# Two-layer hybrid trunk in split fp32: more block products by the seven-product scheme, their block sums by DMA, output projections by pairs of column blocks

## The chip, the cores and the metric

The kernel runs on one core of one Trainium2 chip. The metric is the device time of one execution in microseconds (us). Lower is better.

## The reference

What is computed, for 256 tokens (two tiles of 128, here called t = 0 and 1), a model width of 2048 and a hidden width of 5632, all in float32:

```
for layer in range(2):
    h = rmsnorm(x, g_mix[layer])
    if layer == 0:
        p = h @ w_in_ab                      # 2048 -> 3072
        a = gmlp_mixer(p[..., :2048])        # gelu, norm, 128-token spatial gating
        b = multi_scale_pool(p[..., 2048:])  # trailing means over 2, 4, 8, 16 tokens
        mix = concatenate([a, b]) @ w_out_ab # 2048 -> 2048
    else:
        mix = mla(h, ...)                    # attention over low-rank q and kv, ending in o @ w_out_c
    x = x + mix
    h = rmsnorm(x, g_ffn[layer])
    x = x + (silu(h @ w_gate) * (h @ w_up)) @ w_down   # 2048 -> 5632 -> 2048
out = rmsnorm(x, g_final)
```

## The kernel before

**Split products.** TensorE multiplies in a rounded 32-bit format, so every weight tile is split in two: ACT copies it to its rounded part `wh` (L105) and DVE subtracts to get the rest `wl` (L106). Activations are split in the same way. One product of a 128x128 activation block with a 128x512 weight block is three matmuls (L211, L212, L213 in `token_product`): hi by wh, hi by wl, lo by wh.

**Quads.** In the feed-forward network (FFN) the weights come as quads of 2048 columns (1 MiB): two blocks of 128 rows of the product by two blocks of 512 columns, b11, b12, b22, b21. With the two token tiles of the left side, a quad is a product of 2x2 blocks by 2x2 blocks. Done plainly ("eight") it is 8 block products, 24 matmuls. Done by the scheme of Strassen and Winograd ("seven") it is 7 block products, 21 matmuls, which go to eight PSUM banks: c11, c12, c21, c22 (pool "mm") and p1, p6, p5, p7 (pool "sm"), joined by DVE adds when the column pair ends. A seven needs sums of blocks: on the left s1, s2, s4 (made once, in `split_pair`), on the right t13 = (b11+b12, b12+b22), 1024 columns wide, and t2, t4 (512 each, L253). `SEVEN` names the quads (3, 5, 6 and 7 of the eight of a column pair of gate and up) that go by seven products, `SEVEN_DOWN` those of down: 3 and 5 of eight, in the last part 3 of six.

**Where t13 comes from.** For quads in `SUMMED` (3, 6, 7 of gate/up) `sums_of` makes it with two DMAs on GpSimd's queue into one of two `t13` buffers: L573 writes src[:, :1024], L574 adds src[:, 512:1536] (512 KB each). The second waits for the first to land, and a first waits until its buffer has been read for the last time, by the split of the t13 two sums before (L106, wl<-t). The other sevens get t13 from one DVE add over 1024 columns (L253, sums<-raw).

**The order.** `chunks_of` is a generator over all quads of a layer's FFN. It starts sums up to three quads, and loads and splits up to two quads (`AHEAD`), before they are used. SP issues one 1 MiB load per quad (L579) into one of three `raw` buffers. An FFN is three parts of (4, 4, 3) chunks. A chunk is one column pair of gate and up (8 quads), its eviction, SiLU, product `hd`, and transposes (L262), which TensorE does after quads 1 and 2 of the next chunk. After a part's chunks comes down: two column pairs of 8 quads (parts 0 and 1), or one pair of 6 quads and two plain column blocks (part 2). `pair_into` evicts a down pair: the p banks after the last seven quad, c11 to c22 at its end (`evict`).

**The output projections** (`w_o0`, `w_o1`, after the mixer and the attention) go through `token_major`: four plain blocks of 512 columns, each 96 matmuls into two banks. After block 2 `trunk_rstd` (L370 and L371 on DVE, L373 and L377 on GpSimd) makes a normalizing factor from the squares (L321) of 1536 columns; ACT scales the trunk by it (L307) and TensorE transposes it (L262) into the FFN's left side during block 3 and at the start of the FFN.

**The start.** The first mixer needs a per-token factor along the free dimension: L191 sums squares by matmul, GpSimd takes the power (L195, `rtok`) and `spread` (L201) turns it on TensorE.

Of the kernel before, what the change touches and what calls it, by code (L numbers as in the profile page):

```python
# [8 lines left out]
F32 = mybir.dt.float32  # L9
# [5 lines left out]
P = 128  # L15
# [8 lines left out]
SUMMED = (3, 6, 7)  # L24

SEVEN_DOWN = {4: (3, 5), 3: (3,)}
# [9 lines left out]
def trunk(ctx: ExitStack, tc: tile.TileContext, a: dict, out: bass.AP):  # L36
# [86 lines left out]

    def next_pending(n=1):
# [159 lines left out]
    def into_trunk(w, k0, nk, moving, g, sums, chunks=None, scaled=None, pairs=None, pair_into=None):  # L284
# [28 lines left out]
        def evict(c, pss):  # L313
            s = slice(c * 512, (c + 1) * 512)
            for t in range(2):
                add(x[:, t, s], pss[t], x[:, t, s])
            if g is None:
                return
            for t in range(2):
                sq = ev([512])  # L320
                nc.scalar.activation(out=sq, in_=x[:, t, s], func=AF.Square, accum_out=sums[:, t, c:c + 1])  # L321
            if g == "final":
                for t in range(2):
                    nc.vector.tensor_tensor(out=x[:, t, s], in0=x[:, t, s], in1=gfin[:, s], op=ALU.mult)
            elif scaled is None:
                for m in (4 * c, 4 * c + 2):
                    pending.append(lambda m=m: turn(m, lambda t, j: x[:, t, (m + j) * P:(m + j + 1) * P]))
            elif c == 2:
                scaled["by"], scaled["back"] = trunk_rstd(sums[:, :, :3], 1536, back=True)
                for b in range(3):  # L330
                    turn_scaled(b)
            elif c == 3:
                turn_scaled(3)

        if pairs is not None:
            for b in pairs:
                pair_into(2 * b, evict)
        blocks = range(4) if pairs is None else range(2 * len(pairs), 4)
# [117 lines left out]
    PAD = 16  # L456
    st, att, qpool = stage(att=1, qpool=2)
# [22 lines left out]
    def pool_product(g):  # L480
        parts = split_weights(a["w_pool"][:, g * 512:(g + 1) * 512], 512)
        wh, wl, _ = parts[0]
        for i in range(2):
            ps = ps_mm.tile([P, 2 * T], F32, name="mm")
            for k in range(2):
                s = slice((i * 2 + k) * P, (i * 2 + k + 1) * P)
                short_product(ps, wh[:, s], wl[:, s], diff[:, 2 * (g % 2) + k, :], k == 0, k == 1)
            m = 2 * g + i
            split_into(ab[:, 8 + m, :], ps[:, :T], gain("pool", m))

    for g in range(4):
        z = qpool.tile([P, 2, PAD + T], F32, name="qn")
        nc.vector.memset(z[:, :, :PAD], 0.0)
        for i in range(2):
            ps = column(a["w_z0"][2 * g + i], KD, xs)
            if rx is None:
                rx = kept(spread(rtok))
            s = gather_halves(ps)
            nc.vector.tensor_tensor(out=z[:, i, PAD:], in0=s, in1=rx, op=ALU.mult)
        pool_group(g, z)  # L500
        if g:
            pool_product(g - 1)

    for m in range(8):

        wb = ev([2, P])
        nc.scalar.dma_start(out=wb, in_=a["w_s"][m])
# [21 lines left out]
    into_trunk(a["w_o0"], 0, KD, ab, "ffn0", sums, scaled=scaled)  # L529


    def quad_seven(raw, t13=None):

        sums = big.tile([P, 2048], F32, name="sums")
        if t13 is None:
            t13 = sums[:, :1024]
            add(t13, raw[:, 512:1536], raw[:, :1024])
        t2, t4 = sums[:, 1024:1536], sums[:, 1536:]  # L540
# [6 lines left out]
        parts += split_raw(sums[:, 1024:], 1024)  # L547
        return dict(zip(("b22", "b21", "b11", "", "t1", "t3", "t2", "t4"), (block(parts, i) for i in range(8))))
# [5 lines left out]
    def chunks_of(layer, early):  # L554

        wgu, wd, we = (a[f"{n}{layer}"] for n in ("w_gu", "w_d", "w_e"))
        quad = lambda j, seven: "seven" if j in seven else "eight"
        todo = []
        at = 0
        for n in PARTS:  # L560
            for c in range(at, at + n):
                todo += [(wgu[c, j], "summed" if j in SUMMED else quad(j, SEVEN)) for j in range(KD // 2)]
            last = at + n == sum(PARTS)
            for b in range(1 if last else 2):
                todo += [(wd[b, 2 * at + j], quad(j, SEVEN_DOWN[n])) for j in range(2 * n)]
            if last:
                todo += [(we[c, :, i * 512:(i + 4) * 512], "whole") for c in range(2) for i in range(0, 4 * n, 4)]
            at += n

        def sums_of(src):  # L570

            t13 = early.tile([P, 1024], F32, name="t13")
            nc.gpsimd.dma_start(out=t13, in_=src[:, :1024])  # L573
            nc.gpsimd.dma_start(out=t13, in_=src[:, 512:1536], accum_op=ALU.add)  # L574
            return t13

        def load(src, kind, t13):
            raw = raws.tile([P, 2 * SPLIT], F32, name="raw")
            nc.sync.dma_start(out=raw, in_=src)  # L579
            if kind == "whole":  # L580
                return split_raw(raw, 2 * SPLIT)
            return quad_eight(raw) if kind == "eight" else quad_seven(raw, t13)
# [54 lines left out]
    def feed_forward(layer, sums, scaled, g_next):  # L637
# [3 lines left out]
        st, hds, early = stage(hds=2, early=2)  # L641
        chunks = chunks_of(layer, early)
        for part, n in enumerate(PARTS):
# [4 lines left out]
            hforms = hds.tile([P, 2, 2, 3, P] if not final else [P, 1, 2, 4, P], F32R, name="hforms", bufs=1)  # L648
            for c in range(n):
# [17 lines left out]
                for t, (g, u) in enumerate(((e11, e12), (e21, e22))):  # L667
                    nc.scalar.activation(out=g, in_=g, func=AF.Silu, scale=f[:, t:t + 1])
                    h = hds.tile([P, 512], F32, name="hd")
                    nc.vector.scalar_tensor_tensor(out=h, in0=u, scalar=f[:, t:t + 1], in1=g, op0=ALU.mult, op1=ALU.mult)  # L670
                    hd.append(h)
# [12 lines left out]
            def pair_into(c, evict, hid=hid, hforms=hforms, seven_d=seven_d):  # L684
                s0, s1 = slice(c * 512, (c + 1) * 512), slice((c + 1) * 512, (c + 2) * 512)
# [23 lines left out]
            into_trunk(None, 0, 4 * n, hid, g_next if final else None, after, chunks, pairs=range(1 if final else 2), pair_into=pair_into)  # L709
# [3 lines left out]

    sums = feed_forward(0, sums, scaled, "mix1")
# [13 lines left out]
    ckv = big.tile([P, 4, 2 * T], F32R, name="ckv")  # L728
    st, att, qpool = stage(att=1, qpool=2)
# [86 lines left out]
    def values(h, prt):  # L816
# [3 lines left out]
        split_into(os_[:, h, :], o[:, :T])  # L820
# [4 lines left out]
    queries, probs = {}, {}  # L825
# [26 lines left out]
    into_trunk(a["w_o1"], 0, KD, os_, "ffn1", sums, scaled=scaled)  # L852
# [8 lines left out]
def _laid_out(i):  # L861
# [15 lines left out]

    def flat(t):
# [17 lines left out]
    o["w_o0"] = wide(i["w_out_ab"][0])  # L896
# [14 lines left out]
    o["w_o1"] = wide(i["w_out_c"][0])  # L911
    for l in range(2):
# [3 lines left out]

        w = i["w_down"][l].reshape(NF // 2, 2, P, 2, 2, 512)
        o[f"w_d{l}"] = np.ascontiguousarray(np.stack([w[:, 0, :, :, 0], w[:, 0, :, :, 1], w[:, 1, :, :, 1], w[:, 1, :, :, 0]]
                                                     ).transpose(3, 1, 2, 0, 4)).reshape(2, NF // 2, P, -1)
# [28 lines left out]
```

## Time and profile before

| | us |
|---|---|
| time, median of 3 runs (lowest to highest) | 1906.62 (1906.11 to 1909.29) |
| the profiled execution's own time | 1904.91 |
| its span in the trace | 1903.1 |
| busy in the span: TensorE (PE) | 1890.4 (99%) |
| VectorE (DVE) | 1584.0 (83%) |
| ScalarE (ACT) | 1149.7 (60%) |
| GpSimd (POOL) | 103.9 (5%) |

A row of the timeline is: start in us, length in us, engine, source line, operation, output and input by the program's names, shapes, number joined in the row, and in brackets the idle time of the engine before it and what ended it. PEld is TensorE's weight load, which runs beside the matmuls. A matmul row's length (0.39) is longer than its step to the next one, since matmuls are pipelined. For POOL's DMA rows the start is the moment of issue.

### The profile page before, as it was taken

What the parts mean: (1) busy time and instruction counts of PE and PEld (TensorE: products, weight loads), DVE (VectorE), ACT (ScalarE), POOL (GpSimd) and SP (SyncE); (2) the same over time, 40 slices, a digit from 0 to 9 for tenths busy, and PEclk for the clock granted to TensorE, in tenths of its full rate; (3) what the DMA queues carried; (4) which work ended last, traced back from release to release, by engine and by line L of the source; (5) the groups of instructions that cost most, each with busy time, mean ns of one, the idle gap of its engine ahead of it and who ended that gap; (6) DMA issues with size and microseconds to landing.
All of it is one profiled execution on the core that took longest, in us unless ns stands there. A gap on an engine that the chain in (4) does not pass through costs nothing. (4 is left out here: it accounts for less than half of the span.)

```text
span 1903.1 us, 24047 instructions
## 1 busy us (share of the span) xinstructions
PE 1890.4 (99%) x8994; PEld 1586.9 (83%) x8994; DVE 1584.0 (83%) x2067; ACT 1149.7 (60%) x1538; POOL 103.9 (5%) x159
## 2 busy tenths in 40 slices
PE   9999999999999999999999999999999999999998
PEld 8888888888888888888889988888888888888886
DVE  7785589998799987999675755899987999978995
ACT  6554676664567654666555755776655667546663
POOL 0000001000011100000000000000100011001000
PEclk9999999999999999999999999999999999999999
DMA  8567568885688865786455255588866888757863
GB/s 310 200 219 240 183 209 291 274 266 208 215 275 274 293 235 192 251 277 237 177 180 182 93 173 194 191 278 285 262 223 208 261 289 269 255 201 254 264 238 127
DMA packets 74277, 440.19 MB, mean 231 GB/s; under 512 B 8496, under 2 KB 10288, under 8 KB 30256
## 3 DMA queue, kind: packets, MB, share of 16 engines
q1 hardware_dynamic: 53136, 364.93, 52.8%
q0 software_dynamic: 19008, 69.21, 15.4%
q10 hardware_dynamic: 2016, 4.51, 0.7%
q8 instruction: 70, 1.15, 0.2%
q14 instruction: 47, 0.39, 0.1%
HBM read 436.52 MB, written 2.10 MB: 230 GB/s over the span
## 5 line engine op out<-in xcount | busy, mean ns | idle before, releaser
L105 ACT ACTIVATE wh<-raw 128x1024 fp32r<-128x1024 f32 (+1 forms) x692 | 669.6, 986 | 470.2 <-PE mm L213 312.3
L106 DVE TENSOR_TENSOR wl<-raw,wh 128x1024 fp32r<-128x1024 f32 (+1 forms) x692 | 772.4, 1133 | 165.8 <-ACT wh L105 163.6
L211 PE MATMUL mm<-wh,xs 128*128 128x512 f32 x880 | 344.0, 391 | 0.7 <-ACT ev L252 0.7
L212 PE MATMUL mm<-wl,xs 128*128 128x512 f32 x880 | 342.5, 389 | 0.0
L213 PE MATMUL mm<-wh,xs 128*128 128x512 f32 x880 | 342.2, 389 | 0.0
L211 PE MATMUL mm<-wh,hid 128*128 128x512 f32 x852 | 333.3, 391 | 0.4 <-ACT ev L252 0.3
L213 PE MATMUL mm<-wh,hid 128*128 128x512 f32 x852 | 332.0, 390 | 0.0
L212 PE MATMUL mm<-wl,hid 128*128 128x512 f32 x852 | 331.7, 389 | 0.0
L105 ACT ACTIVATE wh<-sums 128x1024 fp32r<-128x1024 f32 x146 | 154.8, 1060 | 102.1 <-DVE sums L253 58.4
L106 DVE TENSOR_TENSOR wl<-sums,wh 128x1024 fp32r<-128x1024 f32 x146 | 177.8, 1221 | 28.6 <-ACT wh L105 24.8
L211 PEld LDWEIGHTS mm<-wh,xs 128*128 128x128 f32 x880 | 165.2, 188 | 35.0 <-ACT ev L252 1.2
L213 PEld LDWEIGHTS mm<-wh,xs 128*128 128x128 f32 x880 | 165.2, 188 | 34.3
L212 PEld LDWEIGHTS mm<-wl,xs 128*128 128x128 f32 x880 | 165.3, 188 | 33.6
L211 PEld LDWEIGHTS mm<-wh,hid 128*128 128x128 f32 x852 | 160.0, 188 | 33.7 <-ACT ev L252 0.8
L213 PEld LDWEIGHTS mm<-wh,hid 128*128 128x128 f32 x852 | 160.0, 188 | 33.2
L212 PEld LDWEIGHTS mm<-wl,hid 128*128 128x128 f32 x852 | 160.1, 188 | 32.5
L135 PE MATMUL mm<-xs,wh 128*128 128x512 f32 x375 | 133.8, 399 | 0.0
L106 DVE TENSOR_TENSOR wl<-t,wh 128x1024 fp32r<-128x1024 f32 x66 | 80.6, 1222 | 36.2 <-ACT wh L105 36.2
L136 PE MATMUL mm<-xs,wl 128*128 128x256 f32 x375 | 104.8, 280 | 0.0
L105 ACT ACTIVATE wh<-t 128x1024 fp32r<-128x1024 f32 x66 | 70.0, 1060 | 35.6 <-PE mm L213 29.8
L253 DVE TENSOR_TENSOR ev<-sm,ev 128x512 f32<-128x512 f32 x130 | 83.4, 682 | 2.4 <-ACT ev L252 2.4
L573 POOL DMA_DIRECT2D t<-in_w_gu x66 | 38.9, 590 | 835.2 <-DVE wl L106 718.0
(237 smaller groups left out, 2649.4 us busy)
## 6 DMA issues: line engine op xcount, KB each, us to landing
raw<-in_w_gu SPq DMA_DIRECT2D x176, 1024.0 KB, 5.9
raw<-in_w_d SPq DMA_DIRECT2D x76, 1024.0 KB, 4.9
t<-in_w_gu POOLq DMA_DIRECT2D x132, 512.0 KB, 6.8
raw<-in_w_o SPq DMA_DIRECT2D x32, 1024.0 KB, 4.9
raw<-in_w_e SPq DMA_DIRECT2D x12, 1024.0 KB, 4.9
raw<-in_w_v SPq DMA_DIRECT2D x10, 1024.0 KB, 6.6
raw<-in_w_z SPq DMA_DIRECT2D x8, 1024.0 KB, 4.9
raw<-in_w_u SPq DMA_DIRECT2D x8, 1024.0 KB, 4.9
```

The lines of the kernel that those rows point to most:

```text
L105: nc.scalar.activation(out=wh[:, :m], in_=raw[:, o:o + m], func=AF.Copy)
L106: nc.vector.tensor_tensor(out=wl[:, :m], in0=raw[:, o:o + m], in1=wh[:, :m].bitcast(F32), op=ALU.subtract)
L135: nc.tensor.matmul(ps, lhsT=wh, rhs=mv, start=first, stop=False)
L136: nc.tensor.matmul(ps[:, :T], lhsT=wl, rhs=mv[:, :T], start=False, stop=last)
L211: nc.tensor.matmul(ps, lhsT=hi, rhs=wh, start=first, stop=False)
L212: nc.tensor.matmul(ps, lhsT=hi, rhs=wl, start=False, stop=False)
L213: nc.tensor.matmul(ps, lhsT=lo, rhs=wh, start=False, stop=last)
L253: add = lambda out, p, q: nc.vector.tensor_tensor(out=out, in0=p, in1=q, op=ALU.add)
L573: nc.gpsimd.dma_start(out=t13, in_=src[:, :1024])
```

## The change

- `SEVEN_DOWN` gets one more quad per column pair: 3, 5 and 6 of eight, and 3 and 4 of six.
- Both output projections go by pairs of column blocks, as down does, with quads 4 and 6 (layer 0) or 6 (layer 1) of eight as sevens (`SEVEN_OUT`). Their weights are laid out in quads, and their t13 comes from a DVE add.
- Every seven quad of the FFN, in gate/up and in down, gets its t13 by the two DMAs. A third t13 buffer is the first half of the tile `sums`, which used to be taken anew for each seven; t2 and t4 always use its second half. Of a summed quad SP loads only three quarters, with two DMAs (512 KB and 256 KB), since b12 is not used alone.
- A pair is evicted at its end: first the four adds of c11 to c22, then the p banks.
- `trunk_rstd` of the output projections runs after the first pair, over 1024 columns instead of 1536.
- `hd` is written in place. The loads of `w_s` move from ACT's queue to GpSimd's. The first `spread` comes after the second column of `w_z0` instead of during the first.

```diff
-SUMMED = (3, 6, 7)
-
-SEVEN_DOWN = {4: (3, 5), 3: (3,)}
+
+
+SEVEN_OUT = ((4, 6), (6,))
+SEVEN_DOWN = {4: (3, 5, 6), 3: (3, 4)}
...
-            nc.tensor.matmul(ps, lhsT=wh, rhs=mv, start=False, stop=True)
+            done.append(nc.tensor.matmul(ps, lhsT=wh, rhs=mv, start=False, stop=True))
...
+            complete(c)
+
+        def complete(c):
+            s = slice(c * 512, (c + 1) * 512)
...
-            elif c == 2:
-                scaled["by"], scaled["back"] = trunk_rstd(sums[:, :, :3], 1536, back=True)
-                for b in range(3):
+            elif c == 1:
+                scaled["by"], scaled["back"] = trunk_rstd(sums[:, :, :2], 1024, back=True)
+                for b in range(2):
                     turn_scaled(b)
-            elif c == 3:
-                turn_scaled(3)
-
-        if pairs is not None:
-            for b in pairs:
-                pair_into(2 * b, evict)
-        blocks = range(4) if pairs is None else range(2 * len(pairs), 4)
+            elif c > 1:
+                turn_scaled(c)
 
+        def pair_into(c):
+
+            s0, s1 = slice(c * 512, (c + 1) * 512), slice((c + 1) * 512, (c + 2) * 512)
+
+            def between(j, cs, ps):
+                if begin is not None:
+                    begin(j)
+
+            cs, (p1, p6, p5, p7) = quads(nk // 2, seven, moving, forms, chunks, between)
+
+            for i, ps in enumerate(cs):
+                y = x[:, i // 2, (s0, s1)[i % 2]]
+                add(y, ps, y)
+            u2 = copy(p6)
+            add(x[:, 0, s0], p1, x[:, 0, s0])
+            add(u2, p1, u2)
+            add(x[:, 0, s1], p5, x[:, 0, s1])
+            sub(x[:, 0, s1], x[:, 0, s1], u2)
+            add(u2, p7, u2)
+            add(x[:, 1, s0], x[:, 1, s0], u2)
+            add(x[:, 1, s1], p5, x[:, 1, s1])
+            sub(x[:, 1, s1], x[:, 1, s1], u2)
+            complete(c)
+            complete(c + 1)
...
+            if i == 1:
+                split_pair(ab[:, 7 + m:9 + m, :], both, oforms[:, SEVEN_OUT[0].index((8 + m) // 2)])
...
-            ps = column(a["w_z0"][2 * g + i], KD, xs)
+            waiting.append((i, column(a["w_z0"][2 * g + i], KD, xs)))
             if rx is None:
-                rx = kept(spread(rtok))
-            s = gather_halves(ps)
-            nc.vector.tensor_tensor(out=z[:, i, PAD:], in0=s, in1=rx, op=ALU.mult)
+                if i == 0:
+                    continue
+                with tc.issue_after(done[-1].ins):
+                    rx = kept(spread(rtok))
...
-        nc.scalar.dma_start(out=wb, in_=a["w_s"][m])
+        nc.gpsimd.dma_start(out=wb, in_=a["w_s"][m])
...
+    def quad_seven(raw, t13=None, t24=None):
+
+
+
         if t13 is None:
-            t13 = sums[:, :1024]
+            sums = big.tile([P, 2048], F32, name="sums")
+            t13, t24 = sums[:, :1024], sums[:, 1024:]
             add(t13, raw[:, 512:1536], raw[:, :1024])
...
-                todo += [(wgu[c, j], "summed" if j in SUMMED else quad(j, SEVEN)) for j in range(KD // 2)]
+                todo += [(wgu[c, j], "summed" if j in SEVEN else "eight") for j in range(KD // 2)]
-                todo += [(wd[b, 2 * at + j], quad(j, SEVEN_DOWN[n])) for j in range(2 * n)]
+                todo += [(wd[b, 2 * at + j], "summed" if j in SEVEN_DOWN[n] else "eight") for j in range(2 * n)]
...
+    def out_weights(w, seven):
+        return [(w[b, j], "seven" if j in seven else "eight") for b in range(2) for j in range(KD // 2)]
...
+            both = big.tile([P, 2048], F32, name="sums")
+            begun_sums = []
 
-            t13 = early.tile([P, 1024], F32, name="t13")
+            begun_sums.append(0)
+            t13 = early.tile([P, 1024], F32, name="t13") if len(begun_sums) % 3 else both[:, :1024]
             nc.gpsimd.dma_start(out=t13, in_=src[:, :1024])
             nc.gpsimd.dma_start(out=t13, in_=src[:, 512:1536], accum_op=ALU.add)
             return t13
 
         def load(src, kind, t13):
             raw = raws.tile([P, 2 * SPLIT], F32, name="raw")
-            nc.sync.dma_start(out=raw, in_=src)
+            if kind == "summed":
+
+                nc.sync.dma_start(out=raw[:, 1024:], in_=src[:, 1024:])
+                nc.sync.dma_start(out=raw[:, :512], in_=src[:, :512])
+            else:
+                nc.sync.dma_start(out=raw, in_=src)
...
-                def between(j, cs, ps):
-                    if j != seven_d[-1]:
-                        return
-                    if final and g_next == "final":
-                        nonlocal gfin
-                        gfin = big.tile([P, D], F32, name="sums")
-                        nc.scalar.dma_start(out=gfin, in_=a["g_final"].broadcast_to([P, D]))
-                    p1, p6, p5, p7 = ps
-                    u2 = copy(p6)
-                    add(x[:, 0, s0], p1, x[:, 0, s0])
-                    add(u2, p1, u2)
-                    add(x[:, 0, s1], p5, x[:, 0, s1])
-                    sub(x[:, 0, s1], x[:, 0, s1], u2)
-                    add(u2, p7, u2)
-                    add(x[:, 1, s0], x[:, 1, s0], u2)
-                    add(x[:, 1, s1], p5, x[:, 1, s1])
-                    sub(x[:, 1, s1], x[:, 1, s1], u2)
-
-                (c11, c12, c21, c22), _ = quads(2 * n, seven_d, hid, hforms, chunks, between)
-                evict(c, (c11, c21))
-                evict(c + 1, (c12, c22))
...
-    into_trunk(a["w_o1"], 0, KD, os_, "ffn1", sums, scaled=scaled)
+    into_trunk(None, 0, KD, os_, "ffn1", sums, chunks_of(out_weights(a["w_o1"], SEVEN_OUT[1])), scaled, 2,
+               SEVEN_OUT[1], oforms)
```

In all, TensorE has 48 matmuls fewer, DVE has 104 instructions more although 34 of its 40 adds over 1024 columns are gone, and GpSimd issues 232 DMAs for sums instead of 132.

GpSimd's row of instructions for one chunk of gate and up, the second of layer 0 (t_... is a t13 buffer, in_w_gu the weights of gate and up). Before:

```order
L573 DMA t_2569<-in_w_gu 128x1024
L574 DMA t_2569<-in_w_gu 128x1024
L573 DMA t_2729<-in_w_gu 128x1024
L574 DMA t_2729<-in_w_gu 128x1024
L573 DMA t_2766<-in_w_gu 128x1024
L574 DMA t_2766<-in_w_gu 128x1024
```

And in the changed kernel:

```order
L630 DMA t_2656<-in_w_gu 128x1024
L631 DMA t_2656<-in_w_gu 128x1024
L630 DMA sums<-in_w_gu 128x1024
L631 DMA sums<-in_w_gu 128x1024
L630 DMA t_2816<-in_w_gu 128x1024
L631 DMA t_2816<-in_w_gu 128x1024
L630 DMA t_2853<-in_w_gu 128x1024
L631 DMA t_2853<-in_w_gu 128x1024
```

A chunk has four sums on the queue instead of three, one after the other as before, and the second of them goes to the tile `sums`.

DVE at the place where the trunk's factor is made in the output projection of layer 0 (x is the trunk, mm and sm the PSUM banks, L106 and L107 the weight split, L370 or L403 the reduction for the factor). Before:

```order
L106 TENSOR_TENSOR wl<-raw,wh 128x1024 x8
L253 TENSOR_TENSOR x<-mm,x 128x512 x2
L106 TENSOR_TENSOR wl<-raw,wh 128x1024
L370 TENSOR_REDUCE rstd_s<-tsum 128x2
L371 TENSOR_SCALAR rstd_s<-rstd_s 128x2
L106 TENSOR_TENSOR wl<-raw,wh 128x1024 x2
L279 TENSOR_TENSOR xs<-ev,xs 128x2x256 x2
```

And in the changed kernel, from the add of the last of the four banks on:

```order
L257 TENSOR_TENSOR x<-mm,x 128x512
L257 TENSOR_TENSOR x<-sm,x 128x512 x2
L258 TENSOR_TENSOR x<-x,ev 128x512
L107 TENSOR_TENSOR wl<-raw,wh 128x1024
L257 TENSOR_TENSOR ev<-sm,ev 128x512
L107 TENSOR_TENSOR wl<-raw,wh 128x1024
L257 TENSOR_TENSOR x<-x,ev 128x512
L258 TENSOR_TENSOR x<-x,ev 128x512
L107 TENSOR_TENSOR wl<-raw,wh 128x1024 x2
L403 TENSOR_REDUCE rstd_s<-tsum 128x2
L257 TENSOR_TENSOR sums<-raw 128x1024
L404 TENSOR_SCALAR rstd_s<-rstd_s 128x2
```

Where two adds stood ahead of the reduction, all adds of a pair stand now, with weight splits among them, and a block sum stands between the reduction and the scalar step behind it.

TensorE at the first `spread` (L201, now L205; L191 sums the squares, L135 and L136, now L139 and L140, are a column's products). Before:

```order
L423 MATMUL mm<-wl,xs 128x512
L424 MATMUL mm<-wh,xs 128x512
L191 MATMUL sm<-ones,hid 128x1 x2
L201 MATMUL sm<-ident,rtok 128x128 x2
L135 MATMUL mm<-xs,wh 128x512
L136 MATMUL mm<-xs,wl 128x256
L135 MATMUL mm<-xs,wh 128x512
```

And in the changed kernel:

```order
L139 MATMUL mm<-xs,wh 128x512
L140 MATMUL mm<-xs,wl 128x256
L136 MATMUL mm<-xs,wl 128x256
L137 MATMUL mm<-xs,wh 128x512
L205 MATMUL sm<-ident,rtok 128x128 x2
L139 MATMUL mm<-xs,wh 128x512
L140 MATMUL mm<-xs,wl 128x256
L139 MATMUL mm<-xs,wh 128x512
L140 MATMUL mm<-xs,wl 128x256
```

The turn of rtok has left its place right behind the sums of squares, and stands at the end of the second column.

## Rows read from the trace of the kernel before

**Rows 1.** The page: busy time of the engines, and DMA queues.

```profile
PE 1890.4 (99%) x8994; PEld 1586.9 (83%) x8994; DVE 1584.0 (83%) x2067; ACT 1149.7 (60%) x1538; POOL 103.9 (5%) x159
...
q1 hardware_dynamic: 53136, 364.93, 52.8%
q0 software_dynamic: 19008, 69.21, 15.4%
```

**Rows 2.** Windows: length, busy PE, PEld, DVE, ACT, POOL, clock, DMA share, GB/s.

```profile
295.20:336.90 41.70, 41.70 (x190) 34.62 (x189) 39.17 (x46) 27.38 (x35) 4.21 (x6) 1.00 0.88 278
420.30:462.60 42.30, 42.30 (x188) 35.02 (x187) 37.40 (x43) 21.25 (x24) 0.00 (x0) 1.00 0.65 235
```

**Rows 3.** Timeline of PE: matmuls of a plain block, transposes in a chunk.

```profile
215.63 0.39 PE L211 MATMUL mm<-wh,hid 128*128 128x512 f32 x1
...
217.67 0.39 PE L211 MATMUL mm<-wh,hid 128*128 128x512 f32 x1
...
294.04 1.03 PE L262 MATMUL sm<-ident,hd 128*128 128x128 f32 x8
```

**Rows 4.** Timeline of PE: the first spread.

```profile
51.91 0.71 PE L201 MATMUL sm<-ident,rtok 128*128 128x128 f32 x4 [1.05 <-POOL rtok L195]
```

**Rows 5.** Groups by form: a weight split and a block sum on DVE.

```profile
L106 DVE TENSOR_TENSOR wl<-raw,wh 128x1024 fp32r<-128x1024 f32 x578 | 695.2, 1221 | 149.1 <-ACT wh L105 147.1
...
L253 DVE TENSOR_TENSOR sums<-raw 128x1024 f32<-128x1024 f32 x40 | 48.9, 1222 | 3.9 <-DMA raw<-in_w_gu 3.6
```

**Rows 6.** Timeline of POOL: issues of the sums' DMAs.

```profile
277.38 0.84 POOL L574 DMA_DIRECT2D t<-in_w_gu  x1 [3.72 <-DMA t<-in_w_gu]
278.31 0.56 POOL L573 DMA_DIRECT2D t<-in_w_gu  x1
288.62 0.86 POOL L574 DMA_DIRECT2D t<-in_w_gu  x1 [9.75 <-DMA t<-in_w_gu]
296.62 0.56 POOL L573 DMA_DIRECT2D t<-in_w_gu  x1 [7.14 <-DVE wl L106]
304.00 0.85 POOL L574 DMA_DIRECT2D t<-in_w_gu  x1 [6.83 <-DMA t<-in_w_gu]
...
1235.68 0.85 POOL L574 DMA_DIRECT2D t<-in_w_gu  x1 [3.76 <-DMA t<-in_w_gu]
...
1248.51 0.86 POOL L574 DMA_DIRECT2D t<-in_w_gu  x1 [11.38 <-DMA t<-in_w_gu]
...
1278.92 0.86 POOL L574 DMA_DIRECT2D t<-in_w_gu  x1 [5.36 <-issue]
...
1287.34 0.84 POOL L574 DMA_DIRECT2D t<-in_w_gu  x1 [7.00 <-DMA t<-in_w_gu]
...
1781.28 0.85 POOL L574 DMA_DIRECT2D t<-in_w_gu  x1 [3.85 <-DMA t<-in_w_gu]
...
1793.33 0.84 POOL L574 DMA_DIRECT2D t<-in_w_gu  x1 [10.64 <-DMA t<-in_w_gu]
```

**Rows 7.** The tile t: landing times of its 132 DMAs.

```profile
DMA to landing us min/median/max: 3.9/6.8/13.1
```

**Rows 8.** Timeline of DVE in one chunk: t13 of quad 3, of quad 7.

```profile
295.10 1.22 DVE L106 TENSOR_TENSOR wl<-t,wh 128x1024 fp32r<-128x1024 f32 x1
...
316.63 0.68 DVE L253 TENSOR_TENSOR sums<-t,raw 128x512 f32<-128x512 f32 x1
```

**Rows 9.** Timeline of all engines: end of block 2, first output projection.

```profile
216.71 1.28 DVE L253 TENSOR_TENSOR x<-mm,x 128x512 f32<-128x512 f32 x2
...
219.51 0.16 DVE L370 TENSOR_REDUCE rstd_s<-tsum 128x2 f32<-128x6 f32 x1
...
220.02 0.71 POOL L373 TENSOR_TENSOR rtok<-rstd_s,mhalf 128x2 f32<-128x2 f32 x1 [59.77 <-DVE rstd_s L371]
...
220.92 1.32 ACT L307 ACTIVATE ev<-x,rtok 128x512 f32<-128x512 f32 x2
...
222.44 0.81 PE L262 MATMUL sm<-ident,ev 128*128 128x128 f32 x6
```

More of the change, by code (lines that the diff above doesn't have):

```diff
@@ L282, in split_pair, with into_trunk @@
             nc.vector.tensor_tensor(out=q[:, 1], in0=f, in1=q[:, 0].bitcast(F32), op=ALU.subtract)
-    def into_trunk(w, k0, nk, moving, g, sums, chunks=None, scaled=None, pairs=None, pair_into=None):
+    def into_trunk(w, k0, nk, moving, g, sums, chunks=None, scaled=None, pairs=0, seven=(), forms=None,
+                   begin=None):
         def turn(m, src):
@@ L488, in pool_product @@
             m = 2 * g + i
-            split_into(ab[:, 8 + m, :], ps[:, :T], gain("pool", m))
+            if (8 + m) // 2 not in SEVEN_OUT[0]:
+                split_into(ab[:, 8 + m, :], ps[:, :T], gain("pool", m))
+                continue
+            if i == 0:
+                both = ev([2, T])
+            nc.scalar.activation(out=both[:, i, :], in_=ps[:, :T], func=AF.Copy, scale=gain("pool", m))
+            if i == 1:
+                split_pair(ab[:, 7 + m:9 + m, :], both, oforms[:, SEVEN_OUT[0].index((8 + m) // 2)])
     for g in range(4):
@@ L493, in trunk @@
         nc.vector.memset(z[:, :, :PAD], 0.0)
+        waiting = []
         for i in range(2):
-            ps = column(a["w_z0"][2 * g + i], KD, xs)
+            waiting.append((i, column(a["w_z0"][2 * g + i], KD, xs)))
             if rx is None:
-                rx = kept(spread(rtok))
-            s = gather_halves(ps)
-            nc.vector.tensor_tensor(out=z[:, i, PAD:], in0=s, in1=rx, op=ALU.mult)
+                if i == 0:
+                    continue
+                with tc.issue_after(done[-1].ins):
+                    rx = kept(spread(rtok))
+            for j, ps in waiting:
+                s = gather_halves(ps)
+                nc.vector.tensor_tensor(out=z[:, j, PAD:], in0=s, in1=rx, op=ALU.mult)
+            waiting = []
         pool_group(g, z)
@@ L546, in quad_seven @@
         parts += split_raw(t13, 1024)
-        parts += split_raw(sums[:, 1024:], 1024)
+        parts += split_raw(t24, 1024)
         return dict(zip(("b22", "b21", "b11", "", "t1", "t3", "t2", "t4"), (block(parts, i) for i in range(8))))
@@ L552, in quad_eight, with feed_forward_weights @@
         return dict(zip(("b11", "b12", "b22", "b21"), (block(parts, i) for i in range(4))))
-    def chunks_of(layer, early):
+    def feed_forward_weights(layer):
         wgu, wd, we = (a[f"{n}{layer}"] for n in ("w_gu", "w_d", "w_e"))
-        quad = lambda j, seven: "seven" if j in seven else "eight"
         todo = []
@@ L578, in load @@
             raw = raws.tile([P, 2 * SPLIT], F32, name="raw")
-            nc.sync.dma_start(out=raw, in_=src)
+            if kind == "summed":
[3 more added lines that the diff above has]
+                nc.sync.dma_start(out=raw, in_=src)
             if kind == "whole":
                 return split_raw(raw, 2 * SPLIT)
-            return quad_eight(raw) if kind == "eight" else quad_seven(raw, t13)
+            return quad_eight(raw) if kind == "eight" else quad_seven(raw, t13, both[:, 1024:] if t13 is not None else None)
         count, begun, ready = len(todo), [], []
@@ L640, in feed_forward @@
         at = 0
-        st, hds, early = stage(hds=2, early=2)
-        chunks = chunks_of(layer, early)
+        st, hds, early = stage(hds=1, early=2)
+        chunks = chunks_of(feed_forward_weights(layer), early)
         for part, n in enumerate(PARTS):
@@ L712, in feed_forward @@
         return after
+    into_trunk(None, 0, KD, ab, "ffn0", sums, chunks_of(out_weights(a["w_o0"], SEVEN_OUT[0])), scaled, 2,
+               SEVEN_OUT[0], oforms)
+    outs.close()
     sums = feed_forward(0, sums, scaled, "mix1")
@@ L819, in values @@
         nc.tensor.matmul(o[:, P:T], lhsT=vt[:, 1, h * P:(h + 1) * P], rhs=prt[:, T:384], start=False, stop=True)
-        split_into(os_[:, h, :], o[:, :T])
+        if h // 2 not in SEVEN_OUT[1]:
+            split_into(os_[:, h, :], o[:, :T])
+            return
+        if h % 2 == 0:
+            both.append(ev([2, T]))
+        nc.scalar.activation(out=both[-1][:, h % 2, :], in_=o[:, :T], func=AF.Copy)
+        if h % 2:
+            split_pair(os_[:, h - 1:h + 1, :], both.pop(), oforms[:, SEVEN_OUT[1].index(h // 2)])
     q_tiles = columns(a["w_q"], 4, 24, cq)
-    queries, probs = {}, {}
+    queries, probs, both = {}, {}, []
     for p in range(10):
```

46 lines of the change are left out of this document (30 added, 16 removed).

## The prediction

> **What bounds the kernel now.** The page comes first: TensorE is busy for 1890.4 of 1903.1 us, 99%, and DVE for 83% [rows 1]. So time can be won only by fewer matmuls or by closing the 13 us of gaps; a faster DVE, ACT or DMA gives nothing by itself. The windows then show where a new wait could arise. In a stretch as long as one chunk of gate and up, 41.70 us, TensorE never rests, but DVE is busy for 39.17 and the DMA engines for 0.88 of the time. In a stretch of down they have more room: 37.40 of 42.30, and 0.65 [rows 2]. So gate and up is where three resources are close to their end at once, and the change touches all three there. The timeline of TensorE gives the unit: nine matmuls from 215.63 to 217.67, 0.2267 us each [rows 3]. Last, GpSimd's row of sums: these DMAs run strictly after one another, and behind a sum another one needs 11.2 us (277.38 to 288.62) [rows 6]. This is the row on which the forecast hangs.
>
> **The change, part by part.**
>
> *Fewer matmuls.* A quad that turns from eight into seven saves 3. Down has 2 pairs of column blocks in each of parts 0 and 1 and one in part 2, so 5 quads per layer, 10 in all; the output projections 2 quads by 2 pairs in layer 0 and 1 by 2 in layer 1, 6 in all. 16 x 3 = 48 matmuls by 0.2267 = **-10.9 us**. Since TensorE sets the pace there, all of it counts, as long as its inputs come in time.
>
> *The start.* TensorE waits 1.05 us for rtok ahead of the first spread [rows 4]. The spread now stands 64 matmuls later, far behind the power that it waits for, while the column's own products need nothing from it: **-1.1 us**. The eviction of the first column waits for the second; that is hidden by matmuls.
>
> *First pair to second pair in the output projections.* Before, transposes stand 24 matmuls behind block 2. DVE begins its two adds at 216.71, the reduction runs at 219.51, the power at 220.02, ACT's copies at 220.92 for 1.32 us, and TensorE does its transposes at 222.44 without a wait [rows 9]. Now DVE has, from the last of the four bank adds to the scalar step behind the reduction: 7 adds or subtractions of 512 columns at 0.64 (two take 1.28), 4 splits at 1.2, the reduction 0.16, a block sum 1.2 and the scalar step of 0.17 [rows 5, 9], 10.8 us together. The power (0.7, with its hand-over 0.8) ends at 11.6, the copies (1.32) at 12.9. The transposes stand 51 matmuls behind the pair's end in the changed kernel, 11.6 us. So they come 1.2 us late, in each of two layers: **+2.4 us**. Nothing, if ACT and DVE run ahead as they do before; 3 us each, if ACT's squares and copies stand behind splits of weights that are themselves late.
>
> *Second pair to the FFN.* The factor is known, and the first transposes stand 48 matmuls (10.9 us) behind the end. Of the list above the reduction and the power fall away: 4.5 of adds, 4.8 of splits and 1.3 of copies are 10.6, with hand-overs about 11.3. I take 0.4 each, **+0.8 us** (0 to 2 each).
>
> *The pair ends of down.* All 12 adds of a pair now come at its end: 12 x 0.64 = 7.7 us on DVE in one lump, 10 times. They are hidden: the next two quads are split already (two are prepared ahead), so the third quad's splits are needed only two quads later, 10.9 us. Cost 0; at most 1 us each, 10 in all, if a split made ahead is not there. The third DMA in that place, and hd written in place, cost no engine anything.
>
> *DVE.* Block sums of 1.22 us [rows 5] leave it: 22 of gate and up (one per chunk) and 18 of down, while 6 come in the output projections. A pair of down loses two of them, and its third seven adds two sums of 512 columns and 1536 more columns of splits: 1.3 + 1.8 - 2.4 = +0.7 us, against 4.9 that are free there [rows 2]. This makes DVE's room in gate and up larger, 39.2 to 37.9 of 41.7, and shows nowhere in the time, for TensorE does not wait there now.
>
> *DMA engines.* A sum takes them 15.4% x 1903 / 66 = 4.4 us, a raw load of 1.05 MB 52.8% x 1903 / 348 = 2.9 us [rows 1]. A chunk gets one sum and four loads lose a quarter: +4.4 - 2.9 = +1.5 us on 36.7 of 41.7, or 0.92. Close, but not the bound. The Trainium skill ("DMA: Bandwidth & Descriptors", Rules for kernel authors) wants 1 MiB or more per DMA for full bandwidth, which speaks against the loads in pieces of 512 and 256 KB; here only the first few loads of the program are that small, so no row in the FFN bears on it.
>
> *The sums on GpSimd's queue.* Four per chunk instead of three, all through one queue, each second DMA waiting for its first to land. In steady state a chunk of 41.7 us has room for four if the pitch p from one second DMA to the next is 10.4 us. Before, p can be read where a sum follows at once: 20 such places, mean 11.4, first 11.2, last 12.0, shortest 8.4, longest 12.8 [rows 6]. That is over 10.4. But a lag does not cost at once. Take the worst sum, that of quad 7. Its buffer is free when the t13 three sums earlier is split (row 295.10), it goes out at 296.62, its second DMA at 304.00 [rows 6, 8], and that lands after the median of 6.8 [rows 7], at 310.8. TensorE wants its fourth product at 322.0 (the chunk began at 283.1: four eights, three sevens and the transposes of 0.87 end at 320.0, and three products take 2.0); less 3.3 us for add, split, add and split, t13 has to be there at 318.7. Margin 7.9 us. With lag 4p - 41.7 added per chunk and four chunks in a part at most (down then lets the queue catch up), the last chunk's sum is three lags late: no delay up to p = 41.7/4 + 7.9/12 = **11.1**. Which p? The lowest bound is two fastest landings, 3.9 + 3.9 = 7.8; the highest the longest pair, 12.8. Measured is 11.4 beside loads of 1 MiB each. Of these, half turn into 768 KB in two pieces, so the load traffic that the sums share the engines with falls to 7/8. Two lone fastest landings need 7.8, so 3.6 of the 11.4 us are contention; 3.6 x 7/8 + 7.8 = 11.0, and if the smaller pieces in front count in proportion (3/4), 10.5. I take **10.8: delay 0**. At 11.4 the lag per chunk is 3.9, and a four-chunk part ends about 3.8 us late; four such parts make 15 us. At 12, four parts and the two of three chunks come to some 53 us; at 12.8, about 104.
>
> The Trainium skill ("DMA: Bandwidth & Descriptors", the anatomy of a DMA from GpSimd) has 2.0 us plus bytes by 436 GB/s, which by my estimate is 3.2 us for 512 KB and 25.7 for four sums, no lag at all. The trace does not agree: 11.4 us for two of them, so the sum goes by the trace.
>
> **Sum:** -10.9 - 1.1 + 2.4 + 0.8 = -8.8 on the profiled execution's 1904.9, so 1896.1. The median lies 1.7 above it: **1897.8 us**, 0.5% faster.
>
> **Rivals.**
>
> *The queue of sums becomes the bound* (the other side). One mechanism: p stays at 11.2 or more with four sums per chunk, t13 of quad 7 comes late, DVE stands at its t13 add, and TensorE waits in the second half of each part's chunks. For it: the mean of 11.4, and the DMA share that rises to 0.92. Against it: smaller loads, a third buffer that lets a first DMA go out earlier, and time to catch up in down, which has one sum in 14 us. Time: 1897.8 + 15 = 1913 at p = 11.4; it eats the whole gain of 8.8 at about p = 11.25; 1920 to 1950 beyond 11.6.
>
> *The pair ends cost as much as the products give.* Output boundaries 3 + 2 us in each layer (10 instead of 3.2) and 1 us at each end in down (10): 1897.8 + 6.8 + 10 = 1914 at the very worst, about 1905 with half of it, which is no change. For it: DVE has its longest lump ever there, and banks of PSUM come free only after it. Against it: two quads of splits ahead.
>
> *The DMA engines become the bound.* A fastest landing of 512 KB lasts 3.9 us [rows 7], its bytes take 2.9 / 2 = 1.45 by the share of the raw loads. If the other 2.4 us held the engines, four more loads and two more sum DMAs per chunk cost 14 us, where 41.7 - 38.2 = 3.5 are free; at half of it still 3.7 us by 22 chunks, 81 us: 1979. Against it: before, 14 DMAs per chunk (8 loads, 6 for sums) already run, and their packets take the 0.88 that the bytes do, not more. The Trainium skill ("DMA: Bandwidth & Descriptors", Queues, rings and completion order) lets engines take turns between queues packet by packet, and so would fill such gaps.
>
> **How the numbers follow.** Forecast 0.60; queue of sums 0.25; pair ends 0.11; DMA engines 0.04. The forecast's own range, from the bounds of the boundaries, is 1893 to 1903. The range for 8 in 10 has to reach into the queue's case, up to p = 11.5: 1893 to 1918. A measurement of this kernel can tell about 0.2%, 3.8 us: faster below 1902.8, slower above 1910.4. Faster: the forecast and a little of the pair ends, 0.63; same: most of the pair ends and the mildest of the queue, 0.13; slower: 0.24.
>
> **What would show it.** Right: TensorE busy for some 1879 us with gaps in FFN below 2 us in all; no wait ahead of the first spread; a wait of 1 to 2 us ahead of the transposes in the second pair of each output projection; pitch of the sums below 11.1 where four follow each other, and DVE's t13 add never waiting for a DMA at quad 7. Wrong: rows of TensorE with idle time ended by wl whose own chain leads to a landing of t13, growing from chunk to chunk in a part (the queue of sums); idle time at the first matmul into a bank behind an add (pair ends); ACT's wh waiting for raw (DMA engines).

## The result, and the profile after

The changed kernel takes **1924.37 us** (median of 9 runs, 1914.55 to 1927.54); the kernel before, run beside it, 1904.24 (median of 9). The ratio is **1.0092, 95% interval 1.0079 to 1.0106**: slower by 0.9%, where 0.5% faster was forecast. 1924.4 also lies above the stated range.

The page of the changed kernel, to be read beside [rows 1]:

```profile
span 1923.4 us, 24532 instructions
...
PE 1890.2 (98%) x8946; PEld 1579.5 (82%) x8946; DVE 1627.3 (85%) x2171; ACT 1189.7 (62%) x1592; POOL 181.9 (9%) x267
...
q1 hardware_dynamic: 69840, 334.53, 48.3%
q0 software_dynamic: 33792, 122.70, 26.5%
...
raw<-in_w_gu SPq DMA_DIRECT2D x88, 1024.0 KB, 7.6
```

48 matmuls are gone, and yet TensorE is busy for the same time and the span is 20.3 us longer. The sums' queue (q0) takes 26.5% of the DMA engines instead of 15.4, and a load of 1 MiB for gate and up lands after 7.6 us; in the kernel before the same line says 5.9:

```profile
raw<-in_w_gu SPq DMA_DIRECT2D x176, 1024.0 KB, 5.9
```

What TensorE waits for, first before, then after (the columns: who waits, for what; us in total, how often, the longest):

```profile
PE mm L211 <- ACT ev L252: 1.1, 2, 0.7
PE sm L90 <- DVE ones L77: 1.1, 1, 1.1
PE sm L201 <- POOL rtok L195: 1.0, 1, 1.0
```

```profile
PE mm L215 <- ACT ev L256: 17.6, 13, 2.7
PE sm L266 <- ACT ev L312: 2.0, 2, 1.7
PE mm L139 <- ACT ckv L473: 1.8, 1, 1.8
```

The first row is the one that grew, from 1.1 to 17.6 us: a bank of the pool mm that ACT has not yet copied out. A step is the time from the start of one matmul to the start of the next. What a step is longer than the usual step of its kind sums to 46.0 us after and 15.7 before, 30.3 more; less 10.9 for 48 matmuls this is 19.4, close to the 20.3 of the spans. Of these 46.0 us, 20.5 lie at the ends of 16 of the 22 chunks of gate and up.

**One such chunk end, step by step.** ACT in the changed kernel, around the end of a chunk:

```profile
535.30 1.05 ACT L106 ACTIVATE wh<-raw 128x1024 fp32r<-128x1024 f32 x1
536.25 0.58 ACT L256 ACTIVATE ev<-mm 128x512 f32<-128x512 f32 x1
536.73 2.00 ACT L106 ACTIVATE wh<-raw 128x1024 fp32r<-128x1024 f32 x2
538.63 0.58 ACT L256 ACTIVATE ev<-mm 128x512 f32<-128x512 f32 x1
541.88 1.06 ACT L106 ACTIVATE wh<-raw 128x1024 fp32r<-128x1024 f32 x1 [2.67 <-DMA raw<-in_w_gu]
542.85 0.58 ACT L256 ACTIVATE ev<-mm 128x512 f32<-128x512 f32 x1
```

and TensorE beside it:

```profile
541.41 0.39 PE L217 MATMUL mm<-wh,xs 128*128 128x512 f32 x1
543.48 0.50 PE L215 MATMUL mm<-wh,xs 128*128 128x512 f32 x1 [1.68 <-ACT ev L256]
...
553.25 0.48 PE L215 MATMUL mm<-wh,xs 128*128 128x512 f32 x1
```

In ACT's order of instructions, splits of the next chunk's weights stand between the evictions. The split at 541.88 belongs to quad 2 of the next chunk, which TensorE begins at 553.25, 11 us later. Its load was issued at 533.35 and landed at 541.78, after 8.4 us. ACT stands for it; behind it in ACT's order stands the copy of a bank that TensorE wants now. So a load that is late for nobody holds TensorE through ACT's order.

The kernel before has the same order, and the load of that quad (issued at 527.98) is just in time:

```profile
533.27 0.58 ACT L252 ACTIVATE ev<-mm 128x512 f32<-128x512 f32 x1
533.78 1.06 ACT L105 ACTIVATE wh<-raw 128x1024 fp32r<-128x1024 f32 x1
534.75 0.58 ACT L252 ACTIVATE ev<-mm 128x512 f32<-128x512 f32 x1
...
1326.14 1.06 ACT L105 ACTIVATE wh<-raw 128x1024 fp32r<-128x1024 f32 x1 [1.68 <-DVE ev L253]
1327.11 0.58 ACT L252 ACTIVATE ev<-mm 128x512 f32<-128x512 f32 x1
...
1327.74 0.50 PE L211 MATMUL mm<-wh,xs 128*128 128x512 f32 x1 [0.74 <-ACT ev L252]
```

At 533.78 the data have been there for 0.1 us. In one chunk, issued at 1318.59, they needed 7.4 us, and there the whole chain stands already in the trace of before: ACT idle for 1.68 (the row names an add long done; the load ended it), TensorE idle for 0.74. Worked out for all 22 loads of this place (quad 2 of each chunk): mean landing 5.4 us before and 7.6 after; ACT's idle time ahead of the split behind each sums to 8.2 us before and 44.3 after.

Why that load takes longer is shown by the DMA engines during its two flights. After (533.35 to 541.78), then before (527.98 to 533.68); packets, MB, share of the engines:

```profile
q1 hardware_dynamic: 403, 1.84, 61.9%
q0 software_dynamic: 236, 0.84, 34.1%
```

```profile
q1 hardware_dynamic: 144, 1.05, 65.6%
q0 software_dynamic: 42, 0.17, 16.5%
```

The loads get about the same share; the sums took 16.5% before and take 34.1% now, and the engines are nearly full. Over the 22 loads the sums take 0.6 us of the engines' time in a flight before and 3.6 after, the loads 3.5 in both. The Trainium skill ("DMA: Bandwidth & Descriptors", Queues, rings and completion order) has the engines take turns between queues packet by packet. No row here shows the turns themselves; it shows only that both queues moved packets in the one flight, 403 and 236.

**The clock.** Behind three of TensorE's waits in this execution the granted clock falls to half, the lower level of 1.2 GHz, for 3.4 us: behind the first column of w_z0 and behind the two longest waits at chunk ends. The windows at the first two places (columns as in [rows 2]):

```profile
53.77:57.18 3.41, 3.41 (x13) 2.92 (x12) 0.33 (x2) 2.70 (x8) 0.23 (x1) 0.50 1.08 358
374.57:377.94 3.37, 3.37 (x10) 2.62 (x8) 3.37 (x6) 1.91 (x3) 0.00 (x0) 0.51 1.00 230
```

At the second, TensorE had stood for 2.45 us up to 373.54 and run for 1 us. Eight matmul steps then take 0.42 us instead of 0.23, 1.6 us lost; the third place, at 675 behind a wait of 2.70 us, the same. At the first, TensorE had stood for 1.77 us up to 52.35, and the loss is 1.5 us. Behind other waits of this execution it did not fall, that of 1.70 us in the first output projection among them.

### The profile page after: what moved, and what is told of

The parts are those of the page before. It is cut to its first block, busy times and chain, and to the rows that moved or that the text cites. A ratio compares the mean times of both kernels' runs of the same rounds, so it can differ in the third digit from the quotient of the medians.

```text
span 1923.4 us, 24532 instructions
## 1 busy us (share of the span) xinstructions
PE 1890.2 (98%) x8946; PEld 1579.5 (82%) x8946; DVE 1627.3 (85%) x2171; ACT 1189.7 (62%) x1592; POOL 181.9 (9%) x267
## 3 DMA queue, kind: packets, MB, share of 16 engines
q0 software_dynamic: 33792, 122.70, 26.5%
## 4 chain that ended last, share of the span: by engine, by line
PE 78%; DVE 8%; DMA 7%; ACT 3%; issue 2%; POOL 0%; SPq 0%; ACTq 0%; POOLq 0%; DVEq 0%
PE mm L215 18%; PE mm L217 18%; PE mm L216 18%; DVE wl L107 5%; DMA raw<-in_w_gu 5%; PE mm L139 5%; PE sm L215 3%; PE sm L216 3%; PE sm L217 3%; ACT wh L106 2%; PE mm L140 2%; PE sm L266 2%; DMA raw<-in_w_d 1%; DVE sums L257 1%; PE mm L145 1%
## 5 line engine op out<-in xcount | busy, mean ns | idle before, releaser
L106 ACT ACTIVATE wh<-raw 128x1024 fp32r<-128x1024 f32 (+1 forms) x692 | 662.2, 976 | 432.5 <-PE mm L217 244.3
L107 DVE TENSOR_TENSOR wl<-raw,wh 128x1024 fp32r<-128x1024 f32 (+1 forms) x692 | 761.1, 1120 | 117.4 <-ACT wh L106 113.3
L215 PE MATMUL mm<-wh,hid 128*128 128x512 f32 x756 | 296.9, 393 | 5.5 <-ACT ev L256 5.4
L216 PE MATMUL mm<-wl,hid 128*128 128x512 f32 x756 | 295.3, 391 | 0.0
L217 PE MATMUL mm<-wh,hid 128*128 128x512 f32 x756 | 295.3, 391 | 0.0
L107 DVE TENSOR_TENSOR wl<-sums,wh 128x1024 fp32r<-128x1024 f32 x166 | 201.3, 1221 | 37.7 <-ACT wh L106 35.8
L106 ACT ACTIVATE wh<-sums 128x1024 fp32r<-128x1024 f32 x166 | 175.1, 1059 | 83.1 <-PE mm L217 41.9
L215 PEld LDWEIGHTS mm<-wh,hid 128*128 128x128 f32 x756 | 142.4, 188 | 36.1 <-ACT ev L256 6.6
L217 PEld LDWEIGHTS mm<-wh,hid 128*128 128x128 f32 x756 | 142.2, 188 | 29.7
L216 PEld LDWEIGHTS mm<-wl,hid 128*128 128x128 f32 x756 | 142.4, 188 | 28.8
L139 PE MATMUL mm<-xs,wh 128*128 128x512 f32 x375 | 135.3, 402 | 1.8 <-ACT ckv L473 1.8
L107 DVE TENSOR_TENSOR wl<-t,wh 128x1024 fp32r<-128x1024 f32 x78 | 95.3, 1222 | 25.2 <-ACT wh L106 25.1
L106 ACT ACTIVATE wh<-t 128x1024 fp32r<-128x1024 f32 x78 | 82.8, 1061 | 42.5 <-PE mm L217 27.8
L140 PE MATMUL mm<-xs,wl 128*128 128x256 f32 x375 | 105.6, 282 | 0.0
L631 POOL DMA_DIRECT2D t<-in_w_gu x60 | 51.6, 860 | 438.2 <-DMA t<-in_w_gu 416.1
```

The source lines that it names most:

```text
L106: nc.scalar.activation(out=wh[:, :m], in_=raw[:, o:o + m], func=AF.Copy)
L107: nc.vector.tensor_tensor(out=wl[:, :m], in0=raw[:, o:o + m], in1=wh[:, :m].bitcast(F32), op=ALU.subtract)
L215: nc.tensor.matmul(ps, lhsT=hi, rhs=wh, start=first, stop=False)
L216: nc.tensor.matmul(ps, lhsT=hi, rhs=wl, start=False, stop=False)
L217: nc.tensor.matmul(ps, lhsT=lo, rhs=wh, start=False, stop=last)
```

## The experiments

Theory A, formed from these rows: packets of the fourth sum fill the engines while quad 2's load is in flight, and ACT's order turns the late load into a wait for banks. The rivals: pieces of 512 and 256 KB are slow (B); the late data themselves are what is missing (C); the sums in down do it (D); two more DMAs on the queue do it, adding or not (E). The forecast's own main rival, t13 late for DVE, needed no run: among DVE's waits in the changed kernel none is for a DMA of t13.

**Three sums per chunk.** Quad 5 of gate and up by DVE's add from a whole load, two t13 buffers, all else as changed. The fourth sum, the third buffer and the pieces of one load go together here:

```diff
-                todo += [(wgu[c, j], "summed" if j in SEVEN else "eight") for j in range(KD // 2)]
+                todo += [(wgu[c, j], "summed" if j in SUMMED else "seven" if j in SEVEN else "eight") for j in range(KD // 2)]
```

> Theory A (packets of the fourth sum take the DMA engines' time while the load of quad 2 of the next chunk runs, ACT stands at that quad's split, and the evictions queued behind it on ACT hold TensorE's banks): with three sums per chunk the load of quad 2 lands in about 5.6 us again instead of 7.6, the 17 waits of TensorE at chunk ends (20.8 us, and 3.4 us of low clock behind two of them) fall below 4 us together, time 1897 to 1902 us. Theory B (the weight loads are slower because they come in pieces of 512 and 256 KB): three of four sevens per chunk are still loaded in pieces, so landing stays above 7 us, time 1915 to 1922 us.

**Evictions first.** Four sums as changed; the next split after a chunk's last eviction is queued behind it on ACT:

```diff
+        if behind:
+            with tc.issue_after(behind.pop().ins):
+                return split_raw(raw, n, step)
...
-                e11, e12, e21, u2 = *(copy(p) for p in cs[:3]), copy(p6)
+                e11, e12, e21, u2 = *(copy(p) for p in cs[:3]), copy(p6, True)
```

> All four evictions of a chunk stand on ACT ahead of the split of quad 2 of the next chunk. Theory A (ACT's order turns a late load into a wait for a bank): the load still takes 7.6 us, but TensorE's waits at chunk ends fall below 3 us together, time 1898 to 1904 us. Theory C (the late data are what is missing, ACT's order only shows it): TensorE waits at quad 2 itself instead, time stays at 1915 to 1925 us.

**Down by DVE.** t13 of down's sevens by DVE adds, in the same three buffers:

```diff
-                todo += [(wd[b, 2 * at + j], "summed" if j in SEVEN_DOWN[n] else "eight") for j in range(2 * n)]
+                todo += [(wd[b, 2 * at + j], "seven" if j in SEVEN_DOWN[n] else "eight") for j in range(2 * n)]
```

> t13 of the sevens of down by DVE adds again, gate and up as in the changed kernel. Theory A: chunk ends inside a part keep their waits (about 13 of 17), those ahead of down lose some, time 1914 to 1922 us. Theory D (the sums in down, which leave the queue no rest, are what fills the engines): nearly all waits go, time below 1904 us.

**Whole loads.**

```diff
-            if kind == "summed":
-                nc.sync.dma_start(out=raw[:, 1024:], in_=src[:, 1024:])
-                nc.sync.dma_start(out=raw[:, :512], in_=src[:, :512])
-            else:
-                nc.sync.dma_start(out=raw, in_=src)
+            nc.sync.dma_start(out=raw, in_=src)
```

> Summed quads are loaded whole, 1 MiB in one DMA, with four sums as in the changed kernel. Theory A (it is the engines' time that counts): 2.9 us more of it per chunk, the load of quad 2 lands in 8 us or more, longer waits at chunk ends, time 1930 to 1950 us. Theory B (pieces are slow): landing near 5.6 us, time below 1910 us.

These four ran on one chip, beside 9 runs of the kernel before at 1905.11. The ratios can be set beside the changed kernel's own, 1.0092:

| | us, median | ratio to before, 95% interval |
|---|---|---|
| three sums | 1899.3 | 0.9966 (0.9953 to 0.9979) |
| evictions first | 1897.8 | 0.9963 (0.995 to 0.9976) |
| down by DVE | 1913.19 | 1.0038 (1.0023 to 1.0053) |
| whole loads | 1924.29 | 1.0112 (1.0084 to 1.014) |

With **three sums** the wait for banks at chunk ends is gone from TensorE's list, and the load lands nearly as it did before. The landing line of its page, for all whole loads of gate and up, then TensorE's longest waits:

```profile
raw<-in_w_gu SPq DMA_DIRECT2D x110, 1024.0 KB, 5.8
```

```profile
PE sm L267 <- ACT ev L313: 2.0, 2, 1.7
PE mm L140 <- ACT ckv L474: 1.8, 1, 1.8
```

The landing of quad 2's load is 5.8 us in the mean (5.4 before, 7.6 in the changed kernel). Theory A's numbers are met. B falls as the main cause: three of four sevens still come in pieces.

With **evictions first** loads stay slow and ACT still stands for them, but TensorE no longer does. The landing line, then the waits of ACT and TensorE:

```profile
raw<-in_w_gu SPq DMA_DIRECT2D x88, 1024.0 KB, 7.2
```

```profile
ACT wh L111 <- DMA raw<-in_w_gu: 42.4, 26, 4.1
...
PE sm L277 <- ACT ev L323: 2.0, 2, 1.7
PE mm L144 <- ACT ckv L484: 1.8, 1, 1.8
PE mm L466 <- ACT wh L111: 1.0, 1, 1.0
```

The total of ACT's row says little, for it is 41.2 us in the kernel before and 50.2 in the changed one. At the place itself, ahead of the split behind quad 2's load, ACT idles for 23.7 us in all, against 44.3 in the changed kernel and 8.2 before, and the load lands after 7.2 us in the mean. No wait for banks at chunk ends is left, and the time, 1897.8, is a little below what A expected. That separates the two links of the chain, and C falls: nobody misses quad 2's data.

**Down by DVE** took about 10 us off by the ratios, a little more than expected of A, and left most of the waits inside the parts (TensorE's waits again):

```profile
PE mm L215 <- ACT ev L256: 10.5, 11, 1.7
```

The three waits ahead of down (5.8 us of lost steps in the changed kernel) and both stretches of low clock at chunk ends are gone; loads of down land in 4.9 us again (median; 8.1 in the changed kernel); gate and up alone keeps the kernel slower than before. D falls as the whole cause and stands as a part of it.

**Whole loads** met neither expectation. A was to give 1930 or more, B below 1910; it came out as the changed kernel did, with a mean landing of quad 2's load of 7.2 us in the execution that was profiled, the fastest of its four (1915.95). So B falls, and A's expectation was wrong in taking every byte on the engines to count alike. Quad 2 is a whole load either way, and in its flights the loads take 3.4 us of the engines, against 3.5 with pieces: the bytes saved by loading three quarters do not show at the moment that counts. The Trainium skill's rule for large loads ("DMA: Bandwidth & Descriptors", Rules for kernel authors) wants 1 MiB or more per DMA for full bandwidth. It is neither borne out nor refuted by this: splitting costs no time here that can be told, and saves none. (In the kernel before, not only the first few loads are that small, as the forecast says, but also four of 256 KB in the mixer, of w_pool; none is in the FFN.)

**Plain second DMA.** The addition in the DMA is left out, so t13 holds one block pair only:

```diff
-            nc.gpsimd.dma_start(out=t13, in_=src[:, 512:1536], accum_op=ALU.add)
+            nc.gpsimd.dma_start(out=t13, in_=src[:, 512:1536])
```

> The second DMA of each sum writes instead of adding, so t13 holds the second block pair alone and the addition is left out; bytes, queue and count of DMAs stay. Theory A (the engines' time of the sums counts): the sums' queue takes 26.5% of the engines for 122.70 MB, 4.2 us per MB, the loads 48.3% for 334.53 MB, 2.8 us; if the plain half costs like a load, the adding half costs twice that, and without it four sums take some 12 us per chunk instead of 18, less than three adding ones. The load of quad 2 then lands in 5.6 to 6.5 us and time is 1897 to 1906 us. Theory E (two more DMAs in the queue are what hurts, adding or not): landing stays above 7 us, time 1915 to 1925 us.

Measured 1901.56 (median of 10 runs, one of which took 8841 us, for a reason that no run shows), ratio 0.9987 (0.9977 to 0.9997), with a mean landing of quad 2's load of 5.8 us. Its sums' queue, then its wait for banks:

```profile
q0 software_dynamic: 33792, 122.70, 18.9%
```

```profile
PE mm L215 <- ACT ev L256: 0.9, 1, 0.9
```

The same packets and bytes take 18.9% of 1897.7 us instead of 26.5% of 1923.4, 359 us instead of 510. So it is the time that the adding takes, not the count of DMAs: E falls.

**A version of the parts that help.** The residue that both good versions show is the start and the output projections. Two kernels put the first column of w_z0 in a bank of the other pool, move the transposes of the output projections' second pair behind its quads 2 and 3, and have the evictions first; one with three sums, one with four.

```diff
-        ps = ps_mm.tile([P, 2 * T], F32, name="mm")
+        ps = ps_sm.tile([P, 2 * T], F32, name="sm") if sm else ps_mm.tile([P, 2 * T], F32, name="mm")
...
-            if j in (1, 2):
+            if j in turn:
                 next_pending(2)
```

> Three sums per chunk and evictions ahead of the split of quad 2, the first column of w_z0 in a bank of the pool sm, transposes of the output projections' second pair behind quads 2 and 3. Expected by what the profiles show: no wait of TensorE at chunk ends, the 1.9 us at the first column and the 1.9 and 0.5 us ahead of the transposes gone: 1893 to 1897 us. If the waits only move (to the spread, or to the quads that need the transposed blocks): 1897 to 1901 us.

> As the last one, but with four sums per chunk and three t13 buffers. Theory A (once ACT's order does not hold the banks, the slower landing is hidden): the same time as with three sums within 3 us, 1893 to 1898 us. If the fourth sum still costs: 1899 us or more.

The last one puts the evictions first in the kernel before, and nothing else:

> The kernel before, with the evictions of a chunk ahead of the split of quad 2. Theory A: only the two waits that the profile before has at chunk ends (0.9 and 0.5 us) can go, 1902 to 1905 us, no change that can be told. If ACT's order cost the kernel before more than its profile shows: below 1900 us.

On one chip, beside 21 runs of the kernel before at 1904.12: with three sums **1892.54**, ratio 0.994 (0.9927 to 0.9952); with four **1892.51**, 0.9936 (0.9922 to 0.995); before with evictions first 1903.85, 0.9995 (0.9986 to 1.0004). The first two come out 0.5 us below the ranges expected, the last within its range. All waits of note are gone from the list with four sums:

```profile
PE sm L91 <- DVE ones L78: 1.1, 1, 1.1
PE sm L277 <- DVE ev L742: 0.5, 1, 0.5
PE sm L849 <- DVE qr L906: 0.5, 2, 0.3
```

So the fourth sum per chunk buys nothing and costs nothing once the order is mended, and the order alone gives the kernel before nothing that can be told.

## Why the prediction was wrong, step by step

**What held.** The 48 matmuls by 0.2267 us: the last two kernels are 11.6 us faster than before, where 10.9 for the matmuls and the 1.0 of the start make 11.9 (13.0 with the 1.1 us that the kernel before waits for banks, which are gone too). The pair ends of down, costed at 0, show no wait above 0.3 us. Second pair to the FFN, +0.8: no wait at all.

**The output projections, +2.4.** Measured 1.86 us of lost steps in layer 0 and 0.50 in layer 1, 2.4 together; but 1.2 were forecast for each, so the total agrees by luck. In layer 0 DVE needed 10.1 us from the last bank add to the scalar step, near the 10.8 forecast; then GpSimd's power, costed at 0.7, took 2.15. Layer 0, then layer 1:

```profile
206.00 2.15 POOL L406 TENSOR_TENSOR rtok<-rstd_s,mhalf 128x2 f32<-128x2 f32 x1 [44.67 <-DVE rstd_s L404]
...
1177.77 0.71 POOL L406 TENSOR_TENSOR rtok<-rstd_s,mhalf 128x2 f32<-128x2 f32 x1 [42.18 <-DVE rstd_s L404]
```

It is 2.15 in the experiments' traces as well; why it takes longer in layer 0 was not tested. The working has a slip there as well, which moves little: 12.9 less 11.6 is 1.3, not 1.2.

**The pitch of the sums, and the rival built on it.** Taken as 10.8; where a sum follows at once it is 10.2 (mean of 48 places in the changed kernel). No wait of DVE in the list is for t13. This rival did not happen.

**The start, -1.1.** Wrong in sign: the lost step is 1.9 us where it was 1.2, and the stretch of low clock behind it costs 1.5 more. The spread moved, but the column behind it needs a bank of the pool mm, and all four hold the first product until ACT's gelu, which needs the same rtok:

```profile
51.61 1.27 ACT L473 ACTIVATE ckv<-mm,rtok 128x512 f32<-128x512 f32 x2 [0.27 <-POOL rtok L199]
```

The old wait had hidden this longer one. A bank of the other pool took it away.

**The step that failed is the one on the DMA engines**: "+4.4 - 2.9 = +1.5 us on 36.7 of 41.7, or 0.92. Close, but not the bound." With it the sum put the wait at chunk ends at nothing; it is 19.1 us. The mean was about right (eight windows about as long as a chunk show 0.83 to 0.92). But within a chunk the engines are not used evenly. In the flight of one load the engines went from 82% to 96%, and that load had a slack of 0.1 us ahead of an ACT that holds TensorE's banks. The forecast looked for slack in t13, the tile that the change makes, and gave it 7.9 us; it never asked which *other* transfer shares the engines with the new one and how much slack that has. The row that would have told, the wait of 0.74 us in the trace of before, was there, one of two, and the forecast does not speak of it. The range failed with it: its upper end came from the pitch of the sums. The rival with full DMA engines, given 0.04, had the right resource, and its sign, ACT's wh waiting for raw, is what the trace shows. Its mechanism was another, a fixed cost per small DMA, and its time of 1979 lies far off.

**The sum, as measured:** of the 30.3 us of longer steps, chunk ends make 19.1 (20.5, less 1.4 before), the low clock 4.7 (1.6 and 1.6 at chunk ends, 1.5 at the start), slower first steps behind the 16 waits some 1.7, the output projections 2.4, the start 0.7. The remaining 1.7 us are spread over small steps and were not traced.

## What to carry to other kernels

When a change adds DMA traffic, list the transfers that fly at the same time and their slack where they are read, in order of program on the reading engine; a busy share averaged over a stage does not tell of the one load that is just in time. An in-order engine that waits for a load early holds everything behind it: put what frees a resource that the bound engine wants ahead of work for later. A wait that is taken away can uncover a longer one for the same thing; look at what the next instruction needs.

## What the runs showed of the hardware

- A DMA that adds into SBUF takes the engines almost twice as long as one that writes. With plain writes only, 232 DMAs of 512 KB took 359 us of the engines, 1.55 us each; with every second one adding they took 510, so an adding one takes 2.85 if a writing one costs the same beside it. The kernel before agrees: its 132, every second one adding, took 293 us, which makes 2.9.
- Three waits of TensorE in the changed kernel (1.77, 2.45 and 2.70 us) were followed by 3.4 us at the lower of its two clocks, beginning 1.1 to 1.4 us after it had started again. Length alone does not decide. With down by DVE the clock fell in the same way behind waits of 1.77 us at the start and of 1.69 in the first output projection; in the changed kernel it did not fall behind the wait of 1.70 us there, nor with three sums per chunk behind either.
